# Strassen sums of an in-projection formed in PSUM, with quads that overlap by two products

## The chip, the cores and the metric

The kernel runs on one NeuronCore of a Trainium2 chip. The metric is the device time of one execution in microseconds. Before the change three runs took 2101.21, 2101.84 and 2105.98 us, so the median is 2101.84 us.

## The reference, cut to what matters

One layer of a hybrid decoder block over 2048 positions of width 1024, in float32. The part that the change touches is the first line, a product of a 2048 x 1024 matrix with a 1024 x 9216 one; its columns then feed everything else.

```python
proj = x @ w_in[l] + b_in[l]                    # 2048 x 9216
q, k, v, g_attn, u_lru, g_lru, gate_logits = jnp.split(proj, SPLIT_POINTS, axis=-1)
# rotary q/k, three dilated attention groups, softmax-weighted sum, times silu(g_attn), @ w_attn_proj
# causal conv on u_lru, gated linear recurrence (scan), times silu(g_lru), @ w_lru_proj
merged = gates[:, :, 0] * y_a + gates[:, :, 1] * y_b
x = layer_norm(DEEPNORM_ALPHA * x + merged @ w_out[l] + b_out[l], ln_gain[l], ln_bias[l])
```

## The kernel before, in words

The kernel has three stages. Stage A, from 0 to about 1438 us in the trace, is the in-projection; it also carries the rotary embedding, the transposes of v, the SiLU gates and the whole recurrence, which run on the other engines while TensorE multiplies. Stage B is the attention together with the recurrence's output projection, stage C the last projections and the layer norm. The change is in stage A alone.

**The products.** The 72 column tiles of w_in (128 features each) are taken in 36 pairs, and the sequence in two halves of two 512-column chunks. A pair and a half make a *quad*: a 2 x 2 block product (two feature tiles by two halves of the 1024 inner dimension, times two halves by two chunks). There are 72 quads, 36 for each half of the sequence. The first two quads of a half are computed plainly, in eight products. The other 68 use a Strassen-Winograd scheme with seven products, numbered 1 to 7. `UNIT` names the weight block of each (A11, A12, S4, A22, S1, S2, S3; the S are sums of A blocks), and `BLK` its block of x (B11, B21, B22, T4, T1, T2, T3; the T are sums of B blocks). Each operand is split into a rounded high part and a low part, and a product is 12 matmuls of 128 x 128 by 128 x 512: four slices of the inner dimension, each high x high, high x low, low x high (`product`, L639).

**Putting them together** (`evacuate`, L656). Every product gets a PSUM bank of its own from a pool of six, and its sums are formed when it is read out. ScalarE copies product 1 to `e`. VectorE forms `u2 = e - P6`, then `u3 = u2 + P7` (with the sign turned for the v columns), then the result `P5 + u3` and `u2 = u2 + P5`, then `e + P2`, `P4 + u3` and `P3 + u2`. `e`, `u2` and `u3` are tiles in SBUF. That is one ScalarE and seven VectorE instructions per quad, in the order 1, 6, 7, 5, 2, 4, 3; in the last quad of a half 1, 2, 6, 7, 4, 5, 3.

**What sets the order of the work.** The order on every engine is the order in which this Python code issues it. A loop over *slots*, one product long, issues in each slot T: the product's 12 matmuls; the events due in this slot (`load_w`, `prep_w`, `sums`, `load_lo`); the steps of the *chains* that may run; and last the readout of the product. A chain is a generator that carries one result tile through its later steps (`qk_chain`, `v_chain`, `silu_chain`, `mg_chain`, `lru`). Each step asks for a time on ScalarE, VectorE and GpSimd, and runs only if the slot's budget (LEN = 2.75 us per engine, with overspending carried over) is not used up; `spend` enters the costs of the rest. `prep_w` makes a weight block's high part on ScalarE (L284) and its low part on VectorE or GpSimd (L240 through `tt`), 4 slots ahead of the product in the first half of the sequence and 3 in the second. In the first half the low parts are stored to DRAM (`wl_scr`), and in the second half `load_lo` brings them back. `added` (L258) lets GpSimd issue DMAs that add one weight block onto another. Weight tiles and results live in 32 SBUF slots of 128 x 512, low parts in four pairs of tiles (`lo`).

**Gates.** `lru` takes a chunk through convolution, two small gate products in PSUM, and a block of ScalarE functions (L514 to L520: tanh on four half tiles or two whole ones, exp, a scaling, tanh; then a square root at L525).

After the last product, `stA.close()` frees stage A's memory. Stage B's first q and k tiles come in during the last quad (`begin`, `qk_parts`, `v_parts`), into the memory of blocks of x that are no longer needed.

Of the kernel before, what the change touches and what calls it, by code (L numbers as in the profile page):

```python
# [31 lines left out]
def hybrid_block_kernel(ctx: ExitStack, tc: tile.TileContext, a: dict, out: bass.AP):  # L32
# [108 lines left out]
    MID, EDGE = (1, 6, 7, 5, 2, 4, 3), (1, 2, 6, 7, 4, 5, 3)  # L141
# [4 lines left out]
    NS, NL = 32, 4  # L146
    TRACE = False
# [77 lines left out]
    def hi_lo(n, kk, src, eng=dve):  # L225

        t = XB[n][:, kk]
        act.activation(t[:, 0], src, AF.Copy)
        eng.tensor_tensor(out=t[:, 1], in0=src, in1=flat(t[:, 0]), op=ALU.subtract)
# [132 lines left out]
    VDVE = .3  # L362
# [27 lines left out]
    def mg_chain(y, sgn, f, c, bank=None):  # L390

        i = f - FT_MA
        if bank is None:
            yield Ask(lag=0, ACT=.66)
        act.activation(y, y if bank is None else bank, AF.Tanh, scale=0.5 * sgn, bias=bh[:, f:f + 1])
        if now["n"] >= base[NQ - 1]:
# [170 lines left out]
    for h in range(2):  # L567
        for p, (kind, f0, f1) in enumerate(seq):
            plan.append((h, ((f0, kind), (f1, kind)), None if p < 2 else EDGE if p == len(seq) - 1 else MID, p, kind))
    NQ = len(plan)  # L570
    ticks = [8 if pl[2] is None else 7 for pl in plan]
    base = [sum(ticks[:s]) for s in range(NQ + 1)]
# [49 lines left out]
    def product(s, j):  # L622
        order = plan[s][2]
        if order is None:
            fi, k, c = PLAIN[j]
            n, x, first, last, end = f"A{fi + 1}{k + 1}", XB[f"B{k + 1}{c + 1}"], k == 0, k == 1, c == 1
        else:
            n, x, first, last, end = UNIT[order[j]], XB[BLK[order[j]]], True, True, True
        if first:
            Q["b"] = ps.tile([P, CH], F32, tag="q", name=f"q{j}_{s}", bufs=6)  # L630
            if order is None:
                Q["b", fi] = Q["b"]
        bank = Q["b"] if order else Q["b", fi]
        h, l = U[s, n]
        i = 0
        for kk in range(4):
            ks = slice(kk * P, (kk + 1) * P)
            for w, xx in ((h, 0), (h, 1), (l, 0)):
                pe.matmul(bank, w[:, ks], x[:, kk, xx], start=(first and i == 0), stop=(last and i == 11))  # L639
                i += 1  # L640
            if i == 6:
                run(pe_late)
# [6 lines left out]

    def evacuate(s, j):  # L650
        half, _, order, _, _ = plan[s]
        b = Q["b"]
        c0, c1 = 2 * half, 2 * half + 1
        if order is None:
            fi, k, c = PLAIN[j]
            if k:  # L656
                result(s, fi, c0 + c, Q["b", fi], None)
            return
        pid = order[j]
        if pid == 1:  # L660
            Q["e"] = take(f"e{s}", F32)
            act.activation(Q["e"], b, AF.Copy)
        elif pid == 2:
            result(s, 0, c0, b, Q["e"])
# [16 lines left out]
        last = {"e": (2, 6), "u2": (3,), "u3": (4, 5)}  # L681
        for n, p in last.items():
            if pid in p and all(order.index(x) <= j for x in p):
                give(Q.pop(n))

    Q = {}
    COST = {1: dict(ACT=.66), 2: dict(DVE=.72), 6: dict(DVE=.72), 7: dict(DVE=.72), 5: dict(DVE=1.45), 4: dict(DVE=.72), 3: dict(DVE=.72)}


# [5 lines left out]
    for s in range(1, NQ):  # L695
        t0 = base[s] - (3 if plan[s][0] else 4)
# [15 lines left out]
        for j in range(7):  # L712
            if plan[s][0] and j % 2 == 0:
                at(t0 + (3 if s == NQ - 1 and j == 6 else j - 1), lambda s=s, j=j: load_lo(s, j))
            at(t0 + j, lambda s=s, j=j: prep_w(s, j))
# [160 lines left out]
    begin = {1: qk_parts(0), 3: v_parts(0), 5: qk_parts(1)}  # L876
    low = NS
    where = [(s, j) for s in range(NQ) for j in range(ticks[s])]
    for T, (s, j) in enumerate(where):
# [3 lines left out]
        if plan[s][2]:  # L883
            spend(**COST[plan[s][2][j]])
# [5 lines left out]
        if s == NQ - 1:  # L890
            for fn in begin.get(j, ()):
                fn()
# [770 lines left out]
```

## Time and profile before

| what | value |
|---|---|
| runs | 2101.21, 2101.84, 2105.98 us (median 2101.84) |
| profiled execution | 2103.79 us, of which the span from first to last instruction is 2102.0 |
| mean granted TensorE clock | 0.997 |
| TensorE busy | 2074.7 us (99%) |
| VectorE, ScalarE, GpSimd busy | 1679.4, 1189.4, 765.3 us |

How to read it: busy times are those of one execution, and a share of the span mixes three stages. Matmuls are pipelined: one takes 0.39 us, but the next starts 0.23 us after it, so a busy TensorE can still be late by small gaps. What ends a gap is named by the semaphore that released the waiting instruction. A line such as L240 is a helper that many steps share, so the tiles' names tell them apart: `q` is a product's PSUM bank, `xB` and `xT` blocks of x, `h..` and `l` the high and low parts of weights, `e`, `u`, `v` the Strassen sums (`v` is also the convolution's tile), `y` a result, `g` a gate bank.

### The profile page before, as it was taken

To read this page: it belongs to the slowest core of one execution; us is meant where nothing else is said; L and a number is where in the kernel's file an instruction comes from. 1 tells how busy PE (TensorE), PEld (TensorE's weight loads), DVE (VectorE), ACT (ScalarE), POOL (GpSimd) and SP (SyncE) were. 2 spreads that over 40 slices of the span, in tenths; PEclk is the share of its full clock that TensorE was granted. 3 is DMA by queue.
4 is the path that set the end of the run, shared out by engine and by line. 5 is a ranking of instruction groups with operands and counts; after the bars stand their busy time and mean duration, and the time that the engine had idled before them with its cause. 6 is when DMAs were issued, how large, how long until landed. Compare 5 with 4: busy or idle time off the path is not lost.

```text
span 2102.0 us, 35297 instructions
## 1 busy us (share of the span) xinstructions
PE 2074.7 (99%) x11877; PEld 1694.6 (81%) x11877; DVE 1679.4 (80%) x2985; ACT 1189.4 (57%) x2462; POOL 765.3 (36%) x685
## 2 busy tenths in 40 slices
PE   9999999999999999999999999999999999999998
PEld 7888888877888888888888788887888877788886
DVE  8788999988988878788887988775667776886667
ACT  6456466467457556668567777776666664321100
POOL 2544654553653301120120111114457678521120
PEclk9999999999999999999999999999999999999999
DMA  7877886976886866666666565669788986774431
GB/s 226 246 229 208 244 253 208 264 226 194 252 250 214 295 203 188 195 196 194 199 205 193 185 224 182 213 200 277 211 217 237 242 226 195 231 237 154 149 100 70
DMA packets 333573, 443.09 MB, mean 211 GB/s; under 512 B 164448, under 2 KB 174720, under 8 KB 330320
## 3 DMA queue, kind: packets, MB, share of 16 engines
q1 hardware_dynamic: 316752, 408.38, 62.7%
q0 software_dynamic: 11744, 23.54, 6.0%
q10 hardware_dynamic: 4896, 8.92, 1.1%
q8 instruction: 94, 1.54, 0.3%
q14 instruction: 87, 0.71, 0.1%
HBM read 289.74 MB, written 150.99 MB: 210 GB/s over the span
## 4 chain that ended last, share of the span: by engine, by line
PE 64%; DVE 4%; DMA 4%; issue 3%; ACT 3%; POOL 2%; SPq 1%; DVEq 0%; POOLq 0%; ACTq 0%
PE q L639 39%; PE yb L1233 5%; PE o L1063 3%; PE z L1540 3%; PE z L1539 3%; PE z L1538 3%; PE pt L1030 2%; PE s L999 2%; PE ya L1506 1%; PE ya L1507 1%; PE ya L1505 1%; PE g L497 1%; PE s L993 1%; DMA atr<-at_scr 1%; SPq L1103 0%
## 5 line engine op out<-in xcount | busy, mean ns | idle before, releaser
L639 PE MATMUL q<-xT,hS 128*128 128x512 f32 x1632 | 504.1, 390 | 0.0
L639 PE MATMUL q<-xT,l 128*128 128x512 f32 x1088 | 424.3, 390 | 2.5 <-DVE l L240 2.5
L639 PE MATMUL q<-xB,hA 128*128 128x512 f32 x1344 | 416.5, 391 | 0.2 <-ACT hA L284 0.2
L639 PE MATMUL q<-xB,l 128*128 128x512 f32 x944 | 368.1, 390 | 0.0
L639 PEld LDWEIGHTS q<-xT,hS 128*128 128x128 f32 x1632 | 305.7, 188 | 66.4 <-issue 3.3
L639 PEld LDWEIGHTS q<-xB,hA 128*128 128x128 f32 x1344 | 252.4, 188 | 56.2 <-issue 4.0
L639 PEld LDWEIGHTS q<-xT,l 128*128 128x128 f32 x1088 | 204.3, 188 | 46.7 <-DVE l L240 4.2
L240 POOL TENSOR_TENSOR sw<-sw,sin 128x512 f32<-128x512 f32 x96 | 155.8, 1629 | 157.1 <-ACT sw L329 87.0
L639 PEld LDWEIGHTS q<-xB,l 128*128 128x128 f32 x944 | 177.6, 188 | 37.4 <-DMA l<-wl_scr 0.3
L240 POOL TENSOR_TENSOR y<-y,h 128x512 f32<-128x512 f32 x28 | 39.6, 1416 | 384.2 <-DVE h L538 339.0
L1015 ACT ACTIVATE pb<-pb 128x192 f32<-128x192 f32 (+1 forms) x384 | 160.6, 421 | 27.4 <-DVE pb L1013 27.2
L639 PE MATMUL q<-xB,hS 128*128 128x512 f32 x544 | 167.9, 390 | 1.0 <-ACT hS L284 1.0
L639 PE MATMUL q<-xT,hA 128*128 128x512 f32 x544 | 168.0, 390 | 0.0
L284 ACT ACTIVATE hS<-S 128x512 fp32r<-128x512 f32 x170 | 108.4, 637 | 83.2 <-DVE S L240 68.0
L284 ACT ACTIVATE hA<-wA 128x512 fp32r<-128x512 f32 x220 | 138.3, 636 | 21.3 <-DMA wA<-in_w_in_dram 5.2
L1233 PE MATMUL yb<-hx,wl 128*128 128x512 f32 x576 | 148.7, 400 | 0.1
L240 POOL TENSOR_TENSOR l<-wA,hA 128x512 fp32r<-128x512 f32 x68 | 108.1, 1590 | 80.0 <-ACT hA L284 51.0
L1233 PEld LDWEIGHTS yb<-hx,wl 128*128 128x128 f32 x576 | 104.9, 188 | 27.9 <-issue 5.9
L639 PEld LDWEIGHTS q<-xB,hS 128*128 128x128 f32 x544 | 102.0, 188 | 22.8 <-ACT hS L284 1.4
L639 PEld LDWEIGHTS q<-xT,hA 128*128 128x128 f32 x544 | 101.9, 188 | 22.0 <-issue 1.1
L1509 POOL TENSOR_TENSOR me<-gA,me 128x512 f32<-128x512 f32 x30 | 47.7, 1606 | 158.4 <-DVE gA L1508 136.0
L328 ACT ACTIVATE sw<-y 64x512 f32<-64x512 f32 x96 | 60.6, 631 | 79.2 <-DVE y L580 72.8
(215 smaller groups left out, 4330.1 us busy)
## 6 DMA issues: line engine op xcount, KB each, us to landing
wA<-in_w_in_dram SPq DMA_DIRECT2D x220, 256.0 KB
wl_scr<-l SPq DMA_DIRECT2D x102, 512.0 KB
l<-wl_scr SPq DMA_DIRECT2D x102, 512.0 KB
wS<-in_w_in_dram SPq DMA_DIRECT2D x102, 256.0 KB
wS<-in_w_in_dram POOLq DMA_DIRECT2D x68, 256.0 KB, 6.5
wlr<-in_w_f_dram SPq DMA_DIRECT2D x64, 256.0 KB
mg_scr<-y SPq DMA_DIRECT2D x59, 256.0 KB
v_scr<-vs SPq DMA_DIRECT2D x48, 256.0 KB
```

What stands on the lines that cost most here:

```text
L240: eng.tensor_tensor(out=out, in0=in0, in1=in1, op=op)
L284: act.activation(heads(h), heads(r, False), AF.Copy)
L328: act.activation(flat(sw)[lo_], flat(rw)[up_], AF.Copy, scale=scale)
L639: pe.matmul(bank, w[:, ks], x[:, kk, xx], start=(first and i == 0), stop=(last and i == 11))
L999: pe.matmul(bank[h][es, b, 0:BW], q[hs, n * P + 64 * e:n * P + 64 * e + 64], k_[hs, at + 64 * e:at + 64 * e + BW], start=True, stop=True)
L1015: act.activation(pp, pp, AF.Exp, scale=-1.0, bias=mm, accum_out=ll)
L1063: pe.matmul(o[hs, 2 * i + b, :], (V[:, kb // 8, kb // 2 % 4, kb % 2] if g == 2 else V[:, kb % 2, kb // 4, kb // 2 % 2])[:, 64 * h:64 * h + ...
L1233: pe.matmul(YB["t"], w[:, a, k], hx(8 * c + k)[:, b], start=(hf == 0 and m == 0), stop=(hf == 1 and m == 11))
L1509: (dve if i in (6, 7) else pool).tensor_tensor(out=ME[c][:, f], in0=ga, in1=ME[c][:, f], op=ALU.add)
L1538: pe.matmul(z, mh[:, k], w[:, 0, hs], start=(k == 0), stop=False)
L1539: pe.matmul(z, mh[:, k], w[:, 1, hs], start=False, stop=False)
L1540: pe.matmul(z, ml[:, k], w[:, 0, hs], start=False, stop=(k == 7))
```

## The change

Three of the seven sums move into PSUM, and neighbouring quads overlap.

- Products 6 and 7 no longer get banks of their own. They add onto product 1's bank: after product 1 ScalarE copies the bank to `e`, after product 6 to `u2`, after product 7 to `u3` (`copied`, at L671 of the changed file). Block T2 is made with its sign turned (`hi_lo`), so that adding product 6 gives what subtracting gave.
- Product 3 adds onto product 5's bank, after VectorE has read that bank with `u3` for its own result (`third`).
- The order in a quad is 1, 2, 6, 5, 7, 4, 3, and the last two products, 4 and 3, are issued between the first ones of the next quad: 1, 2, (4 of the quad before), 6, (3 of the quad before), 5, 7. The first Strassen quad of a half has no quad before it, and the last of a half (`piped` is false) keeps product 3 in a bank of its own.
- VectorE is left with four instructions per quad (results 2, 5, 4 and 3), and ScalarE has three copies where it had one.
- The planner's costs follow (`spend` in place of the table `COST`); a v transpose is entered with 0.9 us in place of 0.3 (`VDVE`); block A22 is loaded later in the first half (`LATE`, 4 slots before it is split); in the last quad the times in `begin` move, and only results of that quad's two feature tiles go out through GpSimd's queue.

```diff
-    MID, EDGE = (1, 6, 7, 5, 2, 4, 3), (1, 2, 6, 7, 4, 5, 3)
+    ORDER = (1, 2, 6, 5, 7, 4, 3)
...
+        if n == "T2":
+            act.activation(t[:, 0], src, AF.Copy, scale=-1.0)
+            dve.scalar_tensor_tensor(out=t[:, 1], in0=src, scalar=-1.0, in1=flat(t[:, 0]), op0=ALU.mult, op1=ALU.subtract)
+            return
...
-    VDVE = .3
+    VDVE = .9
...
+    for h in range(2):
+        where += [(h * len(seq) + p, j) for p in range(2) for j in range(8)]
+        for p in range(2, len(seq)):
+            q = h * len(seq) + p
+            before = p > 2
+            where += [(q, 0), (q, 1)] + [(q - 1, 5)] * before + [(q, 2)] + [(q - 1, 6)] * before + [(q, 3), (q, 4)]
+        where += [(q, 5), (q, 6)]
...
+            last = not (pid in (1, 6) or pid == 5 and piped(s))
+            first = not (pid in (6, 7) or pid == 3 and piped(s))
+            key = s, {6: 1, 7: 1, 3: 3 if first else 5}.get(pid, pid)
         if first:
...
+            Q[key] = ps.tile([P, CH], F32, tag="q", name=f"q{j}_{s}", bufs=6)
+        bank = Q[key]
...
+    def copied(s, n, scale=1.0):
+        t = Q[s, n] = take(f"{n}{s}", F32)
+        act.activation(t, Q[s, 1], AF.Copy, scale=scale)
+        spend(ACT=.62)
...
         if pid == 1:
-            Q["e"] = take(f"e{s}", F32)
-            act.activation(Q["e"], b, AF.Copy)
+            copied(s, "e")
+            if j == 0 and plan[s][3] > 2:
+                third(s - 1)
...
         elif pid == 6:
-            Q["u2"] = take(f"u{s}", F32)
-            tt(dve, Q["u2"], Q["e"], b, ALU.subtract)
+            copied(s, "u2")
         elif pid == 7:
-            Q["u3"] = take(f"v{s}", F32)
-            if plan[s][4] == "v":
-                dve.scalar_tensor_tensor(out=Q["u3"], in0=b, scalar=-1.0, in1=Q["u2"], op0=ALU.mult, op1=ALU.subtract)
-            else:
-                tt(dve, Q["u3"], Q["u2"], b, ALU.add)
+            copied(s, "u3", -1.0 if kind == "v" else 1.0)
         elif pid == 5:
-            result(s, 1, c1, b, Q["u3"])
-            tt(dve, Q["u2"], Q["u2"], b, ALU.add)
+            if not piped(s):
+                tt(dve, Q[s, "u2"], Q[s, "u2"], Q[s, 5], ALU.add)
+                spend(DVE=.72)
         elif pid == 4:
-            result(s, 1, c0, b, Q["u3"])
-        else:
-            result(s, 0, c1, b, Q["u2"])
+            if not piped(s):
+                third(s)
+            result(s, 1, c0, Q[s, 4], Q[s, "u3"])
+            give(Q.pop((s, "u3")))
+        else:
+            result(s, 0, c1, Q[s, 5 if piped(s) else 3], Q[s, "u2"])
+            give(Q.pop((s, "u2")))
+
+    def third(s):
+        result(s, 1, 2 * plan[s][0] + 1, Q[s, 5], Q[s, "u3"])
+        spend(DVE=.72)
...
-            for d, n in ((6, "S1"), (6, "S3"), (4, "A11"), (3, "A22"), (3, "A12")):
+            for d, n in ((6, "S1"), (6, "S3"), (4, "A11"), (3, "A12")):
                 at(t0 - d, lambda s=s, n=n: load_w(s, n))
+            at(when[s, 5] - lead - LATE, lambda s=s: load_w(s, "A22"))
...
-    begin = {1: qk_parts(0), 3: v_parts(0), 5: qk_parts(1)}
+    begin = {1: qk_parts(0), 5: v_parts(0), 7: qk_parts(1)}
```

The next two fences are the order of TensorE's instructions in quad 45 (second half, a v pair) and around it. A row names the PSUM bank, the block of x and the weight; `q1_44` is the bank taken at the second product of quad 44, and further rows of the same product are left out. Before:

```order
L639 MATMUL q0_45_8696<-xB11_6906,hA11_45_8631 128x512 x2
...
L639 MATMUL q1_45_8733<-xT2_7211,hS2_45_8654 128x512 x2
...
L639 MATMUL q2_45_8756<-xT3_7238,hS3_45_8679 128x512 x2
...
L639 MATMUL q3_45_8788<-xT1_7259,hS1_45_8709 128x512 x2
```

After:

```order
L655 MATMUL q0_45_8489<-xB11_6772,hA11_45_8415 128x512 x2
...
L655 MATMUL q1_45_8528<-xB21_6816,hA12_45_8446 128x512 x2
...
L655 MATMUL q5_44_8548<-xT4_7238,hA22_44_8471 128x512 x2
...
L655 MATMUL q0_45_8489<-xT2_7077,hS2_45_8504 128x512 x2
...
L655 MATMUL q3_44_8433<-xB22_6947,hS4_44_8541 128x512 x2
...
L655 MATMUL q3_45_8630<-xT1_7131,hS1_45_8561 128x512 x2
...
L655 MATMUL q0_45_8489<-xT3_7104,hS3_45_8587 128x512 x2
```

What moved: product 6 (xT2) stood right behind product 1 and had a bank of its own. It now writes to product 1's bank, two products later, and product 7 (xT3) follows on the same bank two products after that. Between them stand products 4 and 3 of quad 44.

On ScalarE, ahead of the first copy of quad 45, stands a gate block of the recurrence (`tr`, `ti`, `e1_3`). Before:

```order
L284 ACTIVATE hS1_45_8709<-S1_45_8598 128x512
L514 ACT_TABLE_LOAD
L514 ACTIVATE tr1_3_8718<-g01_3_8617,brh_193 64x512
L514 ACTIVATE tr1_3_8718<-g11_3_8618,brh_193 64x512
L514 ACTIVATE ti1_3_8719<-g01_3_8617,brh_193 64x512
L514 ACTIVATE ti1_3_8719<-g11_3_8618,brh_193 64x512
L518 ACTIVATE e1_3_8720<-tr1_3_8718,sp2n_222 128x512
L519 ACTIVATE e1_3_8720<-e1_3_8720,half_t_208 128x512
L520 ACTIVATE tr1_3_8718<-tr1_3_8718,sp2_194 128x512
L662 ACTIVATE e45_8731<-q0_45_8696 128x512
```

After:

```order
L671 ACTIVATE u344_8487<-q0_44_8296 128x512
L289 ACTIVATE hS2_45_8504<-S2_45_8390 128x512
L537 ACTIVATE tr1_2_8417<-tr1_2_8417,one_t_210 128x512
L519 ACT_TABLE_LOAD
L519 ACTIVATE tr1_3_8513<-g01_3_8457,brh_193 64x512
L519 ACTIVATE tr1_3_8513<-g11_3_8458,brh_193 64x512
L519 ACTIVATE ti1_3_8514<-g01_3_8457,brh_193 64x512
L519 ACTIVATE ti1_3_8514<-g11_3_8458,brh_193 64x512
L523 ACTIVATE e1_3_8515<-tr1_3_8513,sp2n_222 128x512
L524 ACTIVATE e1_3_8515<-e1_3_8515,half_t_208 128x512
L525 ACTIVATE tr1_3_8513<-tr1_3_8513,sp2_194 128x512
L671 ACTIVATE e45_8524<-q0_45_8489 128x512
```

What moved: the copy `e45` stands behind such a block in both. Now the copy of the quad before, `u344`, stands ahead of the block, and TensorE's product 6 waits for `e45`, where before only VectorE did. Of the 204 copies of the changed kernel 13 stand directly behind a block with four half tiles; of the 68 before, five did.

More of the change, by code (lines that the diff above doesn't have):

```diff
@@ L395, in mg_chain @@
         act.activation(y, y if bank is None else bank, AF.Tanh, scale=0.5 * sgn, bias=bh[:, f:f + 1])
-        if now["n"] >= base[NQ - 1]:
+        if c > 1 and f in [x[0] for x in plan[NQ - 1][1]]:
             pool.dma_start(mg_scr[i * P:(i + 1) * P, c * CH:(c + 1) * CH], y)
@@ L568, in hybrid_block_kernel @@
         for p, (kind, f0, f1) in enumerate(seq):
-            plan.append((h, ((f0, kind), (f1, kind)), None if p < 2 else EDGE if p == len(seq) - 1 else MID, p, kind))
+            plan.append((h, ((f0, kind), (f1, kind)), None if p < 2 else ORDER, p, kind))
     NQ = len(plan)
-    ticks = [8 if pl[2] is None else 7 for pl in plan]
-    base = [sum(ticks[:s]) for s in range(NQ + 1)]
+    where = []
+    for h in range(2):
[5 more added lines that the diff above has]
+        where += [(q, 5), (q, 6)]
+    when = {x: t for t, x in enumerate(where)}
+    base = [when[q, 0] for q in range(NQ)] + [len(where)]
     now["last"] = base[NQ - 1]
@@ L626, in product @@
             n, x, first, last, end = f"A{fi + 1}{k + 1}", XB[f"B{k + 1}{c + 1}"], k == 0, k == 1, c == 1
+            key = s, fi
         else:
-            n, x, first, last, end = UNIT[order[j]], XB[BLK[order[j]]], True, True, True
+            pid = order[j]
+            n, x, end = UNIT[pid], XB[BLK[pid]], True
+            last = not (pid in (1, 6) or pid == 5 and piped(s))
+            first = not (pid in (6, 7) or pid == 3 and piped(s))
+            key = s, {6: 1, 7: 1, 3: 3 if first else 5}.get(pid, pid)
         if first:
[L630 to L633, printed above, removed]
+            Q[key] = ps.tile([P, CH], F32, tag="q", name=f"q{j}_{s}", bufs=6)
+        bank = Q[key]
         h, l = U[s, n]
@@ L638, in product @@
             for w, xx in ((h, 0), (h, 1), (l, 0)):
-                pe.matmul(bank, w[:, ks], x[:, kk, xx], start=(first and i == 0), stop=(last and i == 11))
+                pe.matmul(bank, w[:, ks], x[:, kk, xx], start=(first and i == 0), stop=(i == 11), skip_group_check=True)
                 i += 1
@@ L648, in product, with piped @@
                 lo_vacant.append(LO.pop((s, u // 2))[0])
+    def piped(s):
+        return plan[s][3] < len(seq) - 1
+    def copied(s, n, scale=1.0):
+        t = Q[s, n] = take(f"{n}{s}", F32)
+        act.activation(t, Q[s, 1], AF.Copy, scale=scale)
+        spend(ACT=.62)
     def evacuate(s, j):
-        half, _, order, _, _ = plan[s]
-        b = Q["b"]
+        half, _, order, _, kind = plan[s]
         c0, c1 = 2 * half, 2 * half + 1
@@ L656, in evacuate @@
             if k:
-                result(s, fi, c0 + c, Q["b", fi], None)
+                result(s, fi, c0 + c, Q[s, fi], None)
             return
         pid = order[j]
+        spend(DVE={2: .72, 4: .72, 3: .72}.get(pid, 0.0))
         if pid == 1:
-            Q["e"] = take(f"e{s}", F32)
-            act.activation(Q["e"], b, AF.Copy)
+            copied(s, "e")
+            if j == 0 and plan[s][3] > 2:
+                third(s - 1)
         elif pid == 2:
-            result(s, 0, c0, b, Q["e"])
+            result(s, 0, c0, Q[s, 2], Q[s, "e"])
+            give(Q.pop((s, "e")))
         elif pid == 6:
-            Q["u2"] = take(f"u{s}", F32)
-            tt(dve, Q["u2"], Q["e"], b, ALU.subtract)
+            copied(s, "u2")
         elif pid == 7:
-            Q["u3"] = take(f"v{s}", F32)
-            if plan[s][4] == "v":
-                dve.scalar_tensor_tensor(out=Q["u3"], in0=b, scalar=-1.0, in1=Q["u2"], op0=ALU.mult, op1=ALU.subtract)
-            else:
-                tt(dve, Q["u3"], Q["u2"], b, ALU.add)
+            copied(s, "u3", -1.0 if kind == "v" else 1.0)
         elif pid == 5:
-            result(s, 1, c1, b, Q["u3"])
-            tt(dve, Q["u2"], Q["u2"], b, ALU.add)
+            if not piped(s):
+                tt(dve, Q[s, "u2"], Q[s, "u2"], Q[s, 5], ALU.add)
+                spend(DVE=.72)
         elif pid == 4:
-            result(s, 1, c0, b, Q["u3"])
-        else:
-            result(s, 0, c1, b, Q["u2"])
[L681 to L684, printed above, removed]
+            if not piped(s):
+                third(s)
+            result(s, 1, c0, Q[s, 4], Q[s, "u3"])
+            give(Q.pop((s, "u3")))
+        else:
+            result(s, 0, c1, Q[s, 5 if piped(s) else 3], Q[s, "u2"])
[3 more added lines that the diff above has]
+        spend(DVE=.72)
     Q = {}
-    COST = {1: dict(ACT=.66), 2: dict(DVE=.72), 6: dict(DVE=.72), 7: dict(DVE=.72), 5: dict(DVE=1.45), 4: dict(DVE=.72), 3: dict(DVE=.72)}
     events = {}
@@ L712, in hybrid_block_kernel @@
         for j in range(7):
+            t = when[s, j] - lead
             if plan[s][0] and j % 2 == 0:
-                at(t0 + (3 if s == NQ - 1 and j == 6 else j - 1), lambda s=s, j=j: load_lo(s, j))
-            at(t0 + j, lambda s=s, j=j: prep_w(s, j))
+                at(t - (3 if s == NQ - 1 and j == 6 else 1), lambda s=s, j=j: load_lo(s, j))
+            at(t, lambda s=s, j=j: prep_w(s, j))
     for s, pl in enumerate(plan):
@@ L889, in hybrid_block_kernel @@
         run_chains()
[L890 to L892 removed]
+        for fn in begin.get(T - base[NQ - 1], ()):
+            fn()
         evacuate(s, j)
```

11 lines of the change are left out of this document (5 added, 6 removed).

## The prediction

> **What bounds the kernel now.** I read the page first, then busy time by stage, then what TensorE waited for, then what ScalarE and VectorE do around a copy. The page:
>
> ```profile
> span 2102.0 us, 35297 instructions
> ...
> PE 2074.7 (99%) x11877; PEld 1694.6 (81%) x11877; DVE 1679.4 (80%) x2985; ACT 1189.4 (57%) x2462; POOL 765.3 (36%) x685
> ```
>
> TensorE is busy for 99% of the span. Cut at the middle and at the end of the in-projection (stretch, then busy us of PE, PEld, DVE, ACT, POOL):
>
> ```profile
> 0.00:700.00 700.00, 691.18 (x3028) 568.15 (x3029) 615.00 (x775) 401.59 (x653) 350.96 (x275) 1.00 0.79 233
> 700.00:1435.00 735.00, 733.86 (x3256) 596.49 (x3255) 589.67 (x840) 507.89 (x808) 108.15 (x76) 1.00 0.66 205
> ```
>
> In these two stretches TensorE is idle for 8.8 and 1.1 us. The change takes no matmul away, so it can gain only such gaps and what slows matmuls. From the chain of waits, an unbroken run:
>
> ```profile
> 662.02 119.71 PE q L639 x528
> ```
>
> That is 0.2267 us per matmul, so a product's slot of 12 takes 2.72 us. What TensorE waited for in the in-projection (us in total, times, longest), without its wait for the very first operand:
>
> ```profile
> PE q L639 <- DVE l L240: 2.5, 4, 1.2
> PE g L501 <- ACT tr L517: 2.1, 1, 2.1
> PE q L639 <- ACT hS L284: 1.0, 1, 1.0
> PE g L501 <- DVE vl L240: 1.0, 1, 1.0
> PE q L639 <- ACT hA L284: 0.2, 1, 0.2
> ```
>
> Eight waits, 6.8 us. The longest, and the granted clock (third figure from the end) around it:
>
> ```profile
> 496.50 0.39 PE L639 MATMUL q<-xB,l 128*128 128x512 f32 x1
> 498.98 0.50 PE L501 MATMUL g<-vh,gw 128*128 128x512 f32 x1 [2.09 <-ACT tr L517]
> ```
>
> ```profile
> 450.00:500.00 50.00, 46.24 (x198) 36.76 (x197) 45.16 (x53) 26.99 (x47) 21.87 (x17) 0.99 0.69 212
> 500.00:550.00 50.00, 50.00 (x216) 41.31 (x215) 44.05 (x52) 32.20 (x48) 22.54 (x19) 0.97 0.67 210
> ```
>
> From start to start this gap is 2.48 us instead of 0.23, so a wait costs 0.16 more than its idle time. The clock of 0.99 and 0.97 loses a further 0.01 x 50 + 0.03 x 50 = 2.0 us. All in all the waits cost 6.8 + 8 x 0.16 + 2.0 = 10.1 us. That is the most that this change can bring.
>
> **The change: what leaves VectorE.** The three sums (readers of PSUM, 68 each; the third is `v`, 56 of its 68 in this row):
>
> ```profile
> L240 DVE TENSOR_TENSOR u<-e,q 128x512 f32<-128x512 f32 x68 | 46.2, 679 | 6.2 <-PE q L639 6.1
> L240 DVE TENSOR_TENSOR u<-u,q 128x512 f32<-128x512 f32 x68 | 45.9, 676 | 0.0
> ...
> L240 DVE TENSOR_TENSOR v<-u,q 128x512 f32<-128x512 f32 x56 | 38.0, 678 | 5.3 <-PE q L639 4.9
> ```
>
> Per quad 3 x 0.68 = 2.0 us, and 34 x 2.0 = 69 us for each half of the sequence. In the first stretch VectorE falls from 615 to about 546 of 700 us, so its free time grows from 85 to 154. None of this lies on the path that sets the end. It counts by what VectorE delivers late. The waits that VectorE or the gate chain caused (2.5 + 2.1 + 1.0, six of them, all where VectorE is fullest) I let go entirely: 5.6 + 6 x 0.16 + 2.0 = 8.6 us; bounds 0 and 10.1. The two waits for ScalarE's `hS` and `hA` stay.
>
> **What ScalarE gains.**
>
> ```profile
> L662 ACT ACTIVATE e<-q 128x512 f32<-128x512 f32 x68 | 40.2, 591 | 37.3 <-PE q L639 22.5 <-issue 8.7 <-DVE l L240 5.5
> ```
>
> Two more copies per quad: 2 x 34 x 0.59 = 40 us per half, so 402 + 40 = 442 of 700 us and 508 + 40 = 548 of 735. There is room on average; what counts is when a copy comes. Today TensorE never waits for it. After the change product 6 waits for the copy `e`, product 7 for `u2`, and the next quad's product 4 for `u3`, because it takes over the bank. Each has two slots, 2 x 2.72 = 5.44 us, from the end of the product that it copies. Behind a waiting product all later matmuls are queued, the gates' too.
>
> A calm place first: last matmul of product 1, then its copy.
>
> ```profile
> 789.26 0.39 PE L639 MATMUL q<-xB,l 128*128 128x512 f32 x1
> ...
> 789.69 0.60 ACT L662 ACTIVATE e<-q 128x512 f32<-128x512 f32 x1 [0.99 <-PE q L639]
> ```
>
> Done 790.29 - 789.65 = 0.64 us after the product. Now a bad one in the first half:
>
> ```profile
> 444.70 0.39 PE L639 MATMUL q<-xB,l 128*128 128x512 f32 x1
> ...
> 445.81 5.45 DVE L240 TENSOR_TENSOR l<-wS,hS 128x512 fp32r<-128x512 f32 x1
> ...
> 452.56 0.63 ACT L328 ACTIVATE sw<-y 64x512 f32<-64x512 f32 x1 [4.70 <-DVE y L580]
> ...
> 453.85 0.60 ACT L662 ACTIVATE e<-q 128x512 f32<-128x512 f32 x1
> ```
>
> The copy stands behind `sw` on ScalarE, `sw` waits for a result of VectorE, and VectorE sits in one subtraction for 5.45 us. The copy is done at 454.45, 9.36 us after its product (445.09). With the new order TensorE would have stood 9.36 - 5.44 = 3.9 us. How often: shortest, median and longest of such instructions, against those that leave.
>
> ```profile
> L240 DVE TENSOR_TENSOR l<-wS,hS x35: 674/693/5446, 53.0 to 712.3; 128x512 fp32r<-128x512 f32 x35
> ```
>
> ```profile
> L240 DVE TENSOR_TENSOR u<-e,q x68: 646/680/699, 56.7 to 1427.9; 128x512 f32<-128x512 f32 x68
> ```
>
> ```profile
> L240 DVE TENSOR_TENSOR l<-wS,hS 128x512 fp32r<-128x512 f32 x35 | 42.0, 1201 | 14.0 <-ACT hS L284 13.7
> ```
>
> The last row's mean is 35 x (1.201 - 0.693) = 17.8 us above the median, some four stretches of 4.75 us in this group. I count eight over all groups (my estimate). The sums that leave were never stretched (longest 699 ns), so the stretches stay. By the Trainium skill (SBUF — State Buffer, section "Who interferes with whom") a VectorE instruction with two SBUF inputs contends with GpSimd's reads, and one with at most one SBUF input doesn't. The trace agrees: `u<-e,q` reads one of its inputs from PSUM. If instead the stretches went with VectorE's load, the next term would be zero.
>
> Price of a stretch after the change: a calm copy plus a stretch is 0.64 + 4.75 = 5.39 us, just inside 5.44. The other 4.0 us of the 9.36 were arrears that VectorE already had. With nearly twice the free time I keep a tenth, 0.4 us each: 8 x 0.4 = 3.2 us; bounds 0 and 8 x 3.9 = 31.
>
> In the second half a gate block does it:
>
> ```profile
> 1225.61 0.39 PE L639 MATMUL q<-xB,l 128*128 128x512 f32 x1
> ...
> 1226.07 0.63 ACT L284 ACTIVATE hS<-S 128x512 fp32r<-128x512 f32 x1
> ...
> 1233.14 0.60 ACT L662 ACTIVATE e<-q 128x512 f32<-128x512 f32 x1
> ```
>
> ScalarE worked from 1226.07 to 1233.74 without a pause, and the copy came 7.74 us after its product, 2.3 too late. Had it begun with product 1's slot, 2.72 us before 1226.00, it would have come 1223.28 + 7.67 - 1226.00 = 4.95 us after, in time. In the new order 13 copies stand right behind such a block. For three (the first copies of quads 45, 53, 69) the copy of the quad before stands ahead of it and holds the block until that product is done, 0.6 us more, with a prep and a scaling between. I take 1.0 us for these three and none for the other ten: 3.0 us; bounds 0 and 13 x 2.3 = 30.
>
> **The rest.** VectorE's `third` reads product 5's bank and must be done three slots (8.2 us) after product 7, and product 3's result as soon; both are later than a calm VectorE needs. T2 with its sign turned is the same number of instructions. `VDVE` and the budgets only move chains. A22's DMA is issued four slots (10.9 us) before its split, as A11's is today, so it costs nothing while SP is on time; if not, ScalarE waits and a copy with it. The lo pairs are held longer, so SP's `load_lo` stands nearer to the product that frees a pair, still some three slots ahead of use. The first q and k tiles of stage B are asked for seven slots ahead of the end instead of five; TensorE did not wait for them. After the last product stands one VectorE result as before. All zero, a microsecond either way for the seam.
>
> **Sum.** -8.6 + 3.2 + 3.0 = -2.4 us. The profiled execution took 2103.79 us (span 2102.0 and 1.8 around it), so it would take 2101.4. It lies 1.95 above the median of the runs, 2101.84, on which I set the forecast: 2099.4 us.
>
> **The rivals.** A measurement of this kernel can tell about 0.3%, 6.3 us, from no change.
>
> *The copies are nearly always in time* (faster). Both new terms vanish with the arrears, and the old waits go: -8.6 to -10.1, so 2091.7 to 2093.2 us. For it: in the calm row the copy is done in 0.64 us. Against it: the stretches and blocks are still there. Chance 0.27.
>
> *TensorE is held by ScalarE's queue* (slower). Mechanism: a copy, at two slots' distance, behind `sw` or a gate block. If arrears stay as they are, eight stretches at 3.9 and the three blocks at 2.3 give 38 us, less the 8.6 that goes: +30, so 2131. But a stop of TensorE lets the others catch up, and half of the 38 gives +10, 2112 us. It decides from 15 us of new waits on, 8.6 + 6.3. For it: ScalarE's share in the second half rises to 75%. Against it: VectorE, behind which ScalarE waited in the bad row, loses a tenth of its load. Chance 0.24. On the clock the Trainium skill (TensorE: Matmul & The Clock Gate, section "What's actually happening") gives an idle window of about 3.4 us before the clock is halved. By it short new waits cost only themselves. The trace doesn't bear that out: the clock fell around a wait of 2.09 us. So a new wait of that length may cost up to 2 us more, which this case contains.
>
> *The change doesn't do what it says*: TensorE's copies are bound elsewhere, and neither old nor new waits move. Then 2101.8, within the bound; chance 0.05, beside 0.44 for the forecast.
>
> **How the numbers follow.** Faster is the first rival, 0.27; slower the second, 0.24; the forecast and the third rival lie within 0.3%, 0.49. The forecast's own range is 2095.5 to 2108. The whole range reaches down to the largest gain, 10.1 us, and a microsecond for the seam (2091), and up to the halved second rival (2112); beyond it I leave a tenth.
>
> **What would show it.** Right: in the in-projection's first half TensorE's waits for `l` and for the gates are gone, VectorE is busy for about 546 us there, and new waits of TensorE for `e`, `u` copies come to some 6 us, a few times, each behind a VectorE stretch or a gate block. Wrong: these waits sum to over 15 us, or there are none; the old waits for `l` remain; or matmuls in unbroken runs are no longer 0.2267 us apart.

## The result, and the profile after

The changed kernel takes 2124.98 us (median of four runs, 2124.47 to 2129.15); beside it the kernel before took 2103.91. The ratio is 1.0102, with a 95% interval of 1.0078 to 1.0126: 1.0% slower, where 2099.4 us had been forecast. The profiled execution took 2124.82 us, 21.0 more than that of before (2103.79).

The page of the changed kernel:

```profile
span 2123.0 us, 34909 instructions
...
PE 2079.2 (98%) x11877; PEld 1695.2 (80%) x11877; DVE 1598.3 (75%) x2783; ACT 1253.8 (59%) x2598; POOL 754.1 (36%) x684
```

VectorE has 202 instructions fewer and ScalarE 136 more, as the change says. The two stretches of the in-projection:

```profile
0.00:700.00 700.00, 677.37 (x2943) 553.14 (x2944) 571.55 (x669) 421.75 (x704) 324.06 (x268) 0.99 0.76 226
700.00:1435.00 735.00, 729.43 (x3235) 592.33 (x3234) 545.99 (x739) 543.50 (x879) 122.04 (x81) 1.00 0.65 203
```

In the same 1435 us TensorE gets through 2943 + 3235 = 6178 matmuls, before it was 6284. The 106 that are missing are 106 x 0.2267 = 24 us of work, so the loss lies here. TensorE is idle for 22.6 us in the first stretch (before: 8.8) and 5.6 in the second (1.1). What it waited for in the in-projection:

```profile
PE q L655 <- ACT u L671: 12.3, 9, 2.3
PE q L655 <- ACT e L671: 7.7, 6, 2.3
...
PE q L655 <- DVE y L611: 2.6, 2, 1.3
PE q L655 <- DVE y L245: 1.6, 1, 1.6
PE g L506 <- ACT tr L522: 0.7, 1, 0.7
```

That is 24.9 us in 19 waits, where there were 6.8 in eight. The old waits for `l` and the gates are gone but for 0.7 us; 20.0 us are waits for ScalarE's copies, and 4.2 us in three waits are for VectorE's read of product 5's bank (`third`). And the clock around some of them:

```profile
250.00:300.00 50.00, 47.01 (x200) 37.56 (x199) 39.41 (x44) 26.14 (x45) 20.70 (x18) 0.97 0.80 235
350.00:400.00 50.00, 45.72 (x192) 36.63 (x191) 47.39 (x46) 29.50 (x47) 28.00 (x22) 0.97 0.74 217
...
600.00:650.00 50.00, 48.06 (x206) 38.84 (x205) 38.15 (x43) 31.08 (x51) 26.77 (x22) 0.97 0.75 231
```

Three windows at 0.97 lose 3 x 0.03 x 50 = 4.5 us, before it was 2.0. Together: 18.1 more of waiting, 11 x 0.16 for eleven more waits, 2.5 of clock, 22.4 us, against 21.0 measured. So the *where* is settled by the trace: TensorE waits for copies. But not why they are late: the second half of the sequence, where ScalarE is fullest, holds four of the 19 waits:

```profile
PE q L655 <- ACT e L671: 2.3, 3, 0.9
PE q L655 <- ACT u L671: 1.7, 1, 1.7
```

One place of the first half, on four engines. GpSimd (start, duration in us, what it does, idle time before it):

```profile
268.93 1.32 POOL L245 TENSOR_TENSOR l<-S,hS 128x512 fp32r<-128x512 f32 x1 [9.81 <-ACT hS L289]
270.18 1.74 POOL L263 DMA_DIRECT2D wS<-in_w_in_dram  x2
271.33 1.91 POOL L245 TENSOR_TENSOR l<-S,hS 128x512 fp32r<-128x512 f32 x1
272.59 1.91 POOL L245 TENSOR_TENSOR l<-wS,hS 128x512 fp32r<-128x512 f32 x1
```

Three low parts started within 4 us, after GpSimd had stood idle for 9.8 us: those of S2, of the quad before's S4 and of S3, which is also the order in which ScalarE is given their high parts. The first waited for its high part, and the others came up behind it. VectorE meanwhile:

```profile
270.71 4.34 DVE L417 SCALAR_TENSOR_TENSOR y<-si,y 128x512 f32<-128x512 f32 x1
...
277.24 0.70 DVE L593 SCALAR_TENSOR_TENSOR y<-q,b,e 128x512 f32<-128x512 f32 x1
```

A step whose median is 0.69 us lasts 4.34, until 275.05, half a microsecond after GpSimd's run ended (274.50); the result `y` of product 2 comes at 277.94. ScalarE:

```profile
278.04 0.63 ACT L333 ACTIVATE sw<-y 64x512 f32<-64x512 f32 x1 [6.16 <-DVE y L593]
...
279.87 1.37 ACT L519 ACTIVATE tr<-g,brh 64x512 f32<-64x512 f32 x2
...
284.98 0.60 ACT L671 ACTIVATE u<-q 128x512 f32<-128x512 f32 x1
```

It stands idle for 6.16 us in front of `sw`, a gate block follows, and only then the copy. And TensorE:

```profile
282.93 0.39 PE L655 MATMUL q<-xT,l 128*128 128x512 f32 x1
285.63 0.74 PE L655 MATMUL q<-xT,hS 128*128 128x512 f32 x2 [2.31 <-ACT u L671]
```

So at this place the copy is the last link, behind a gate block and a late result, and GpSimd stands at the start of the chain. And GpSimd's work is not what it was. Its low parts in the first 720 us, before:

```profile
L240 POOL TENSOR_TENSOR l<-wA,hA 128x512 fp32r<-128x512 f32 x68 | 108.1, 1590 | 80.0 <-ACT hA L284 51.0 <-issue 14.6 <-ACT ub L466 3.9
...
L240 POOL TENSOR_TENSOR l<-S,hS 128x512 fp32r<-128x512 f32 x35 | 54.9, 1568 | 109.1 <-ACT hS L284 70.1 <-issue 22.7 <-PE q L639 7.8
L240 POOL TENSOR_TENSOR l<-wS,hS 128x512 fp32r<-128x512 f32 x33 | 48.3, 1462 | 133.5 <-ACT hS L284 99.4 <-issue 18.9 <-PE q L639 10.6
```

and after:

```profile
L245 POOL TENSOR_TENSOR l<-S,hS 128x512 fp32r<-128x512 f32 x65 | 104.4, 1606 | 189.8 <-ACT hS L289 155.3 <-issue 23.6 <-DMA wl_scr<-l 8.2
...
L245 POOL TENSOR_TENSOR l<-wS,hS 128x512 fp32r<-128x512 f32 x33 | 51.7, 1568 | 67.4 <-ACT hS L289 52.1 <-issue 6.5 <-PE q L655 3.9
L245 POOL TENSOR_TENSOR l<-wA,hA 128x512 fp32r<-128x512 f32 x34 | 50.9, 1496 | 72.9 <-ACT hA L289 62.1 <-ACT ub L471 8.3 <-DMA u_scr<-y 1.6
```

Of the weight sums that VectorE forms (`S`) there are nearly twice as many, of those that DMAs add up (`wS`) as many as before, of the plain blocks (`wA`) half. The reason is one line of `prep_w` that the diff doesn't touch: `eng = pool if j % 2 == 0 and plan[s][2] else dve`. It hands every second block *by its place in the order* to GpSimd. With the old order these were A11, S3, A12, S4, with the new one A11, S2, S3, S4. The change swapped S2 for A12 in GpSimd's queue, and the prediction didn't see it.

### The profile page after: what moved, and what is told of

Its sections match the earlier page's. It is cut to its first block, busy times and chain, and to the rows that moved or that the text cites. A ratio compares the mean times of both kernels' runs of the same rounds, so it can differ in the third digit from the quotient of the medians.

```text
span 2123.0 us, 34909 instructions
## 1 busy us (share of the span) xinstructions
PE 2079.2 (98%) x11877; PEld 1695.2 (80%) x11877; DVE 1598.3 (75%) x2783; ACT 1253.8 (59%) x2598; POOL 754.1 (36%) x684
## 4 chain that ended last, share of the span: by engine, by line
PE 58%; DMA 3%; DVE 2%; ACT 1%; POOL 1%; issue 1%; SPq 0%; DVEq 0%; POOLq 0%; ACTq 0%
PE q L655 33%; PE yb L1255 5%; PE o L1085 3%; PE z L1561 3%; PE z L1560 3%; PE z L1562 3%; PE pt L1052 2%; PE s L1021 2%; PE ya L1528 1%; PE ya L1529 1%; PE ya L1527 1%; PE s L1015 1%; PE g L502 1%; DMA atr<-at_scr 1%; DMA V<-v_scr 0%
## 5 line engine op out<-in xcount | busy, mean ns | idle before, releaser
L655 PE MATMUL q<-xT,hS 128*128 128x512 f32 x1632 | 509.9, 394 | 20.1 <-ACT u L671 12.3
L245 POOL TENSOR_TENSOR l<-S,hS 128x512 fp32r<-128x512 f32 x68 | 108.2, 1592 | 201.0 <-ACT hS L289 161.4
L245 DVE TENSOR_TENSOR rp<-y,sw 128x512 f32<-128x512 f32 x64 | 97.9, 1535 | 37.3 <-POOL sw L245 35.8
L655 PEld LDWEIGHTS q<-xT,hA 128*128 128x128 f32 x544 | 101.8, 188 | 22.4 <-issue 1.5
```

Source lines behind the costliest of these rows:

```text
L245: eng.tensor_tensor(out=out, in0=in0, in1=in1, op=op)
```

## The experiments

The theory on record (the second rival of the prediction): ScalarE's queue holds TensorE because products now add onto a bank that must be copied first. The rivals: the order and the overlap do it by themselves; or GpSimd's changed set of low parts does, through VectorE's stretched instructions. In the table the columns are: median, ratio to the kernel before in the same runs (its medians there were 2103.91 to 2105.86 us) with its 95% interval, VectorE instructions of over 3 us, and unbroken runs of GpSimd of over 4 us (less than 0.1 us between its instructions, DMA issues included). Both counts are of those that start in the trace's first 720 us; GpSimd's setup in the first 6 us is left out.

| kernel | us | ratio | VectorE > 3 us | GpSimd > 4 us |
|---|---|---|---|---|
| before | 2103.91 | 1 | 7 | 29 |
| after | 2124.98 | 1.0102 [1.0078, 1.0126] | 16 | 32 |
| e1: own banks | 2148.60 | 1.0203 [1.0183, 1.0224] | 22 | 34 |
| e2: copies first | 2139.33 | 1.0156 [1.0134, 1.0177] | 16 | 31 |
| e3: only product 3 shares a bank | 2133.16 | 1.0135 [1.0112, 1.0158] | 20 | 37 |
| e4: low parts on VectorE | 2094.90 | 0.9950 [0.9932, 0.9969] | 0 | 4 |
| e5: old set on GpSimd | 2097.00 | 0.9951 [0.9937, 0.9966] | 8 | 19 |
| e6: before, low parts on VectorE | 2097.41 | 0.9963 [0.9951, 0.9976] | 5 | 14 |
| e7: e1, low parts on VectorE | 2090.27 | 0.9931 [0.9905, 0.9957] | 0 | 4 |
| e8: VDVE .3 | 2128.42 | 1.0107 [1.0082, 1.0132] | 16 | 30 |
| e9: before, new set on GpSimd | 2113.88 | 1.0049 [1.0031, 1.0066] | 10 | 32 |
| e10: e1, old set on GpSimd | 2099.64 | 0.9976 [0.9966, 0.9986] | 6 | 25 |
| e11: A11, A12, S2, S1 | 2103.11 | 0.9987 [0.9977, 0.9998] | 5 | 20 |
| e12: A11, A22, S4, S3 | 2103.92 | 0.9996 [0.9985, 1.0007] | 4 | 14 |
| e13: A12, S2, S1, S3 | 2109.05 | 1.0019 [1.0009, 1.0029] | 7 | 22 |
| e14: A11, A12, S3, S1 | 2110.42 | 1.0027 [1.0017, 1.0036] | 3 | 25 |
| e15: A11, S2, S3 | 2106.18 | 1.0009 [1.0000, 1.0018] | 6 | 21 |

### e1: a bank for each product

The changed order, overlap and planner, but the sums are formed by VectorE again.

```diff
-            last = not (pid in (1, 6) or pid == 5 and piped(s))
-            first = not (pid in (6, 7) or pid == 3 and piped(s))
-            key = s, {6: 1, 7: 1, 3: 3 if first else 5}.get(pid, pid)
+            first = True
+            key = s, pid
...
-            copied(s, "u2")
+            u = Q[s, "u2"] = take(f"u2{s}", F32)
+            tt(dve, u, Q[s, "e"], Q[s, 6], ALU.add)
+            spend(DVE=.72)
```

(and likewise for product 7 and for `u2 + P5`.)

> The changed kernel with one part undone: order, overlap, planner and loads as changed, but every product has a bank of its own again, and VectorE forms e + P6, u2 + P7 and u2 + P5 as before (with product 6's turned sign). Theory Q (TensorE loses its time at the copies and at the read of product 5's bank, since sums in PSUM make TensorE wait for ScalarE's and VectorE's queues): these waits are gone, TensorE waits in the in-projection for under 8 us besides the first operand, and the time is 2097 to 2108 us. Theory O (the new order, the overlap or the planner is at fault): still over 2115 us, with waits of TensorE for other things.

It took 2148.60 us, 24 more than the changed kernel. TensorE's waits for copies are gone, and longer ones have come, for low parts on VectorE:

```profile
PE q L654 <- DVE l L245: 14.1, 8, 3.6
PE g L506 <- DVE vl L245: 11.1, 4, 3.3
```

The queue theory falls as the root: without shared banks it is slower still. Something in the order makes VectorE late, whatever hands its lateness on.

### e2 and e3: parts of the queue theory

e2 issues the three copies at the head of the slot instead of its end:

```diff
         product(s, j)
+        copy_out(s, j)
         for fn in events.pop(T, []):
```

> The changed kernel with the three copies of a quad issued at the head of their slot on ScalarE, ahead of this slot's weight splits and chain steps, where they stood behind them. Theory Q: a copy is then done within about 0.7 us of its product unless steps of earlier slots are late, TensorE's waits for e and u fall from 20.0 us to under 8, and the time to 2102 to 2112 us. Rival (a copy waits for what ScalarE got from earlier slots, and its place within the slot does not matter): waits of 15 us or more, 2118 to 2128 us; ScalarE, which stops for the product at the head of the slot, may even be later.

2139.33 us, slower than either expectation. The copies' waits did fall, to 0.7 us, but TensorE now waited for VectorE's reads of the banks:

```profile
PE q L655 <- DVE ub L593: 8.4, 4, 4.4
PE q L655 <- DVE y L593: 6.7, 4, 2.8
...
PE q L655 <- ACT u L671: 0.7, 1, 0.7
```

e3 gives products 6 and 7 banks of their own, and only product 3 adds onto product 5's (`first = not (pid == 3 and piped(s))`).

> The changed kernel with products 6 and 7 in banks of their own (VectorE forms e + P6 and u2 + P7 as before), and only product 3 adding onto product 5's bank. VectorE has one sum per quad less than before, ScalarE one copy per quad. Theory Q: no wait for copies; the read of product 5's bank has three slots and may still cost its 4 us; 2098 to 2110 us. Theory O: over 2115 us.

2133.16 us, between the changed kernel and e1. No wait for a copy is left; the largest is for VectorE's read of product 5's bank:

```profile
PE q L654 <- DVE y L611: 11.0, 3, 5.2
```

e2 and e3 say the same as e1: the wait only changes its name.

### e4: all low parts on VectorE

GpSimd makes no low parts in the first half; the planner's cost of one on VectorE is lowered from .93 to .5, so that the chains still get their turns.

```diff
-            eng = pool if j % 2 == 0 and plan[s][2] else dve
+            eng = dve
...
-                spend(DVE=.93)
+                spend(DVE=.5)
```

> The changed kernel with all low parts of weights in the first half made on VectorE; GpSimd, which made four of seven, keeps the rotary products, the gate products and the adding DMAs. VectorE gets 34 x 4 = 136 subtractions of 0.69 us more, but is stretched less. Theory S (the late copies come from VectorE instructions stretched beside GpSimd): VectorE's long instructions become fewer, TensorE's waits for copies and for VectorE fall below 12 us, 2105 to 2115 us. Rival (VectorE's load as such makes the results late): waits rise above 25 us, 2130 us or more.

2094.90 us, faster than even the first theory gave. VectorE has 136 subtractions more and is busy for less:

```profile
0.00:700.00 700.00, 696.78 (x3069) 574.78 (x3070) 560.33 (x824) 441.08 (x728) 149.57 (x144) 1.00 0.80 239
```

That is 824 instructions in 560 us; in the changed kernel 669 took 572. None lasts over 3 us. TensorE's waits before the end of the in-projection are three, behind gate blocks in the second half:

```profile
PE q L655 <- ACT e L671: 2.3, 3, 0.9
```

So the low parts on GpSimd make the copies late. By which way is not told apart: with them go both VectorE's long instructions and its waits for GpSimd's rotary products (`sw`). The planner's entry was changed as well; e5 leaves it alone.

### e5: the old set

The changed kernel with one line, which gives GpSimd the blocks that it had before.

```diff
-            eng = pool if j % 2 == 0 and plan[s][2] else dve
+            eng = pool if n in ("A11", "S3", "A12", "S4") and plan[s][2] else dve
```

> The changed kernel, with GpSimd making the low parts of A11, S3, A12 and S4 in the first half, as in the kernel before; the change's new order had silently given it S2 in place of A12, since the choice goes by the place in the order. Theory G (that swap puts the low part of a weight sum, which comes late, on GpSimd and bunches its work): stretches and waits fall, 2104 to 2114 us. Rival S (any such work on GpSimd stretches VectorE, whichever block it is): 2119 to 2130 us as the changed kernel.

2097.00 us, again faster than expected. The swap is worth the ratio 1.0102 / 0.9951 = 1.015, some 32 us, more than the whole loss. The waits that are left:

```profile
PE q L655 <- ACT e L671: 2.8, 4, 0.9
...
PE q L655 <- ACT u L671: 1.9, 4, 0.8
```

They come to 4.7 us. VectorE's silu step shows the stretches: in the changed kernel (first 720 us)

```profile
L417 DVE SCALAR_TENSOR_TENSOR y<-si,y 128x512 f32<-128x512 f32 x24 | 43.9, 1830 | 0.7 <-ACT y L413 0.7
```

and in e5

```profile
L417 DVE SCALAR_TENSOR_TENSOR y<-si,y 128x512 f32<-128x512 f32 x24 | 19.4, 806 | 0.1
```

### e6 and e7: the same for the kernel before and for own banks

e6 is the kernel before, e7 is e1, each with all low parts on VectorE (cost .3).

```diff
-            eng = pool if j % 2 == 0 and plan[s][2] else dve
+            eng = pool if n in () and plan[s][2] else dve
...
-                spend(DVE=.93)
+                spend(DVE=0.3)
```

> The kernel before, with all low parts of the first half on VectorE (entered with 0.3 us in the planner, so that chains find room). Theory S (stretches beside GpSimd cause the waits, in either kernel): VectorE, though it gets 136 subtractions more, is stretched less, the waits for l and gates go, 2092 to 2100 us. Rival (without the sums in PSUM VectorE has no room for them): TensorE waits for l and for gates over 15 us, 2110 us or more.

> Both edits: own banks and VectorE sums in the new order, and all low parts of the first half on VectorE (0.3 us in the planner). If the loss of the new order (e1_apart) comes through VectorE's stretches, it goes with them: 2093 to 2108 us. If the order, the overlap or the planner costs TensorE time in another way, it stays above 2125 us.

2097.41 and 2090.27 us. e6 shows that most of e4's gain needs nothing of the change: the kernel before gains 0.37% by the same step (e4 0.50%). e7 is the fastest of all, faster than expected, though of its kind e1 was the slowest: the low parts on GpSimd cost the order with own banks a ratio of 1.0203 / 0.9931 = 1.027. TensorE waits for nothing there until the in-projection's end. That e7 beats e4 by 4.6 us isn't settled, since their intervals overlap; e6's overlaps both as well.

### e8: the planner's cost of a transpose

`VDVE` set back to .3.

> The changed kernel with a v transpose entered with 0.3 us again. Theory P (the dearer entry holds chains back and bunches GpSimd's work): 2105 to 2116 us. Rival (the entry only shifts chains by a slot): 2119 to 2132 us as the changed kernel.

2128.42 us: no help. The waits for copies remain:

```profile
PE q L655 <- ACT u L671: 17.5, 12, 3.4
PE q L655 <- ACT e L671: 6.0, 6, 2.2
```

The costs entered for the transposes don't make the copies late.

### e9 and e10: the swap by itself

e9 is the kernel before with the one line `eng = pool if n in ("A11", "S2", "S3", "S4") …`; e10 is e1 with the line of e5.

> The kernel before, with one thing of the changed one: GpSimd makes the low parts of A11, S2, S3 and S4 in place of A11, S3, A12 and S4. Theory H (the fault is that S2's low part, a weight sum's that comes late, stands in GpSimd's queue ahead of the rotary products) gives 2115 to 2130 us with nothing else of the change in it, VectorE waiting for `sw` of GpSimd by some 30 us in the first half and TensorE's waits there above 20 us. Rival N (the swap hurts only where ScalarE's copies hold TensorE, so only with the sums in PSUM or the new order) gives 2101 to 2108 us.

> The changed order and overlap, with a bank for each product and the sums on VectorE again, and with GpSimd making the low parts of A11, S3, A12 and S4 as before the change. The same without the last took 2148.6 us. H: the order by itself is harmless, so 2092 to 2100 us. The rival, that the order by itself costs beside the sums on VectorE: 2115 us or more. Against the changed kernel with the same low parts (2097.0 us) it tells what the sums in PSUM bring when nothing else is wrong: above 2100 they gain, below 2094 they cost.

e9 took 2113.88 us, a ratio of 1.0049: the swap costs without anything else of the change, but 10 us, which lies between the two expectations, 2101 to 2108 and 2115 to 2130. VectorE waits for `sw` by only 6.0 us there, not by some 30, and has ten instructions of over 3 us where it had seven. TensorE's longest waits there are for VectorE's low parts:

```profile
PE q L639 <- DVE l L240: 8.5, 2, 4.7
```

e10 took 2099.64 us, 49 less than e1. So with the old set the order and the overlap are harmless (the rival with 2115 or more falls), and by the ratios the same swap costs 10 us in the old order, 32 in the changed kernel and 48 with the new order and own banks. Against e5 (2097.00) the sums in PSUM bring 2.6 us, with intervals that just touch; e7 and e4 put it the other way round. What the sums in PSUM bring by themselves is not settled.

### e11 to e15: what it is about the set

All five are the changed kernel with another set in that line. First, S2 kept but spread out, and a spread set without it.

> The changed kernel; GpSimd makes the low parts of A11, A12, S2 and S1 (places 0, 1, 3, 5 of each seven slots): S2 stays on GpSimd, and S1 with it, but the parts stand further apart. The changed kernel's are at 0, 3, 4, 6. H (S2 on GpSimd is the fault): 2112 us or more, and VectorE waits for `sw` by 20 us or more. Rival B (the fault is that GpSimd's low parts come in neighbouring slots, 3 with 4 and 6 with 0): below 2100 us, few waits for `sw`.

> The changed kernel; GpSimd makes the low parts of A11, A22, S4 and S3 (places 0, 2, 4, 6 of each seven slots): no S2, S3 and S4 as in the changed kernel. H: 2093 to 2100 us, no long wait for `sw`. B: about the same as with A11, S3, A12 and S4 (2097.0 us) or some us better. If instead any weight sum on GpSimd is the fault, S3 and S4 too: 2110 us or more.

2103.11 and 2103.92 us. My theory that S2's low part alone is the fault falls with e11, where GpSimd makes it and TensorE loses little. The theory of neighbouring slots did no better in its numbers (below 2100 for e11, about 2097 for e12). Then one set with three weight sums and few neighbours, one with few sums and a row of neighbours, and the changed kernel's own without S4.

> The changed kernel; GpSimd makes the low parts of A12, S2, S1 and S3 (places 1, 3, 5, 6 of each seven slots): three weight sums as in the changed kernel, but one pair of neighbouring slots where that had two (3 with 4, 6 with 0). Theory T (three weight sums, whose high parts come late, pile up in GpSimd's queue and run back to back): 2112 us or more. B (neighbouring slots): 2097 to 2106 us.

> The changed kernel; GpSimd makes the low parts of A11, A12, S3 and S1 (places 0, 1, 5, 6): two weight sums, and four slots in a row, 5, 6, 0, 1. T: 2097 to 2106 us. B: 2112 us or more, with GpSimd in more runs of over 4 us than in the changed kernel.

> The changed kernel; GpSimd makes the low parts of A11, S2 and S3 only, and VectorE that of S4, 34 instructions more for it. T and B, both: with the pile of three gone, 2095 to 2105 us. Rival L (VectorE's load decides, and GpSimd's pile is only beside it): no better than 2120 us, since VectorE has 34 x 0.69 = 23 us more to do in the first half.

2109.05, 2110.42 and 2106.18 us. e13 and e14 both lie between what the two theories gave, and e15 a microsecond above what both gave. e5 weighs against the neighbours: its parts stand at places 6, 0, 1 and 4, with two neighbouring pairs as in the changed kernel, and it is the fastest of the sets on GpSimd. e14 weighs against the count of sums: it has two like e5 and takes 13 us more. So neither theory explains the times. e15 shows that VectorE's load isn't it: 34 subtractions more on VectorE, and 19 us less than the changed kernel. The changed kernel, e4, e5, e8 and e11 to e15 differ in GpSimd's set and the planner's costs alone. Over these nine the time goes with the count of unbroken GpSimd runs (last column), from 4 at 2094.9 us over 19 to 25 at 2097.0 to 2110.4, to 30 and 32 at 2128.4 and 2125.0; e12 with 14 at 2103.9 is out of line. It is a correlation. VectorE's long instructions part the slow kernels from the others (16 and more in all that took over 2120 us, at most 10 in the rest), but don't order the rest: e14 has three and takes 2110.4. VectorE's waits for GpSimd in the first 720 us part these nine just as well: 40.1 us in the changed kernel and 45.9 in e8, at most 17.4 in the others. Which property of the set makes the runs long stays open, and so does whether the long instructions or the waits cost more. One rival is untested: another engine for a low part also changes what the planner enters (1.55 us on GpSimd or .93 on VectorE), so chain steps move by some slots. No run keeps the plan and changes the engine alone; e8 shows only that the plan's entry for a transpose doesn't matter.

## Why the prediction was wrong, by its steps

**The step that failed** is "The rest … All zero". Among the things moved the prediction went through `third`, T2, `VDVE`, A22's DMA, the lo pairs and `begin`, and left out what the new order does to a rule that goes by place: which low parts GpSimd makes. That term, put at nothing, is worth some 32 us (e5). It held that "the stretches stay" because the instructions that leave were never stretched. The remaining ones were stretched more: VectorE instructions of over 3 us went from 7 to 16. The sets tell that this is the swap: 8 with the old set (e5), 0 with no low parts on GpSimd (e4). A second of these zeros failed with it. `third` was to be done in time, but product 3 (block B22 with S4, the only product of an `xB` with an `hS`) waited for it by 4.2 us; in e5 it did not wait.

```profile
L655 PE MATMUL q<-xB,hS 128*128 128x512 f32 x544 | 168.3, 391 | 4.2 <-DVE y L611 2.6
```

**Old waits, -8.6 us: right.** Of 6.8 us of waits 0.7 is left, and in e5 none. With the three sums back on VectorE and the old set (e10) TensorE waits for `l` and the gates by 7.1 us, so it is the leaving sums that free them.

**Stretches, 8 x 0.4 = 3.2 us: mis-sized.** If all waits but the gate blocks', the old one and those for `third` are put down to them, it is 24.9 - 2.3 - 0.7 - 4.2 = 17.7 us for sixteen stretches, 1.1 us each. Number and price were both too low. Part of the price is that VectorE now also waits for GpSimd itself. Its waits in the first 720 us, of the changed kernel:

```profile
DVE rp L245 <- POOL sw L245: 31.3, 10, 4.3
...
DVE y L245 <- POOL sw L245: 8.8, 2, 4.4
```

The rotary product `sw` stands in GpSimd's queue behind the low parts; before, no such wait is listed. And ScalarE's for the results that VectorE owes it, first before, then after:

```profile
ACT sw L328 <- DVE y L580: 34.6, 21, 4.7
```

```profile
ACT sw L333 <- DVE y L593: 99.5, 30, 9.3
```

The longest of these waits was 4.7 us and is 9.3, so a copy behind it no longer has room in its 5.44 us. With the old set the term holds: e5 has eight, and 4.7 - 2.3 = 2.4 us of waits beside the gate blocks.

**Gate blocks, 3 x 1.0 us: right.** Three waits for `e` in the second half, 2.3 us and 3 x 0.16 for their restart make 2.8. They stand in e4 too. Of the ten other copies behind a block, put at nothing, one was late: that of 284.98, by 2.31 us, behind a late result as well.

**Sum.** With the old set the profiled execution took 2100.58 us, 3.2 below that of before; the forecast was 2.4 below. That near match is in part luck: it was the slowest of e5's eight executions, and by the ratio of the medians e5 gains some 10 us, as much as the prediction allowed at most. So the direction was right for a kernel that the change is not; the size is not borne out.

**VectorE falls to about 546 us in the first stretch: wrong**, 571.55. Of the 25 us that came back, 20 are in instructions of over 3 us: they take 57.4 us there, before the change 37.2.

**The second rival had the right last link.** TensorE is held by the copies, new waits passed its 15 us, and its 2112 to 2131 holds the result, though with eight stretches where there were sixteen. Its first link, that ScalarE's load and VectorE's old arrears decide, is not what the runs show: e1 has no such copies in TensorE's way and is slower by 24 us, and e5 and e4 keep all copies and have 4.7 and 2.3 us of waits. The text also held that waits of about 2 us cost clock, and they did. Of the in-projection's four waits of 1.9 us or more (2.34 the longest, the first operand aside) three were followed within 1.3 us by 3.41 us at half the clock; the fourth, of 2.32 us until 203.11, was not:

```profile
200.00:250.00 50.00, 46.33 (x204) 37.73 (x202) 45.64 (x45) 26.06 (x43) 28.57 (x23) 1.00 0.81 231
286.75:290.16 3.41, 3.41 (x10) 2.63 (x9) 3.38 (x6) 2.37 (x3) 0.96 (x1) 0.50 0.48 147
```

The Trainium skill (TensorE: Matmul & The Clock Gate, section "What's actually happening") gives an idle window of about 3.4 us before the clock is halved; the waits here were shorter, so here the measurement decides.

**First rival.** "The copies are nearly always in time" would have been 2091.7 to 2093.2; e4 (2094.90) comes near it, but only with GpSimd's low parts gone.

## What to carry to other kernels

When a change reorders work, search the code for every rule that goes by place in the order (every second block, the first two, the last), and list what each gives to which engine before and after: the diff doesn't show it, a count of each engine's instructions by operands does. Where two engines disturb each other, cost a change by what it does to their overlap, not only by the instructions that it removes. And the wait that ends last names the messenger: follow the chain back until an instruction lasts longer than its own median.

## What the runs showed of the hardware

A VectorE instruction with two SBUF inputs that meets a run of GpSimd instructions doesn't slip in between them: at 270.71 it lasted 4.34 us, across the end of one low part and the start of the next, until the run was over (GpSimd's spans are rough). All sixteen instructions of over 3 us in the changed kernel end 0.56 us (three of them 0.95 to 0.99) after the end of a GpSimd subtraction or product. The nine that met one of these, behind two DMA issues, lasted 3.1 to 3.6 us, the four that met three or four 5.2 to 5.8. The Trainium skill (SBUF — State Buffer, section "Who interferes with whom") has the contention of VectorE instructions with two SBUF inputs and GpSimd's reads, and the trace agrees: all sixteen have two SBUF inputs. That the loss grows with the length of GpSimd's run is what the trace adds. With 136 subtractions moved from GpSimd to VectorE, VectorE's busy time in the first stretch was shorter, 572 to 560 us (e4), and GpSimd's own rotary products faster too: 1735 ns in the changed kernel, 1501 in e4.

```profile
L245 POOL TENSOR_TENSOR sw<-sw,sin 128x512 f32<-128x512 f32 x48 | 81.3, 1735 | 10.7 <-ACT sw L334 7.1 <-DVE y L417 2.7 <-PE q L655 0.9
```

```profile
L245 POOL TENSOR_TENSOR sw<-sw,sin 128x512 f32<-128x512 f32 x48 | 71.8, 1501 | 200.4 <-ACT sw L334 194.7 <-DVE y L245 4.8 <-DVE l L245 0.9
```
